# Cosine-similarity attention with hand-written engine orders: three pairs of heads normalised by head instead of both heads at once, and new orders in the last third

## The chip, the cores and the metric

The kernel runs on one core of one Trainium2 chip. The metric is the device time of one execution in microseconds (us). The engines are TensorE (PE in the profile; its weight loads are PEld), VectorE (DVE), ScalarE (ACT), GpSimd (POOL) and SyncE (SP), which issues most of the DMAs.

## The reference

```python
# Q, K, V: (batch 8, heads 12, seq 512, dim 64), f32; tau = 0.1
Q_norm = Q / (np.linalg.norm(Q, axis=-1, keepdims=True) + 1e-10)
K_norm = K / (np.linalg.norm(K, axis=-1, keepdims=True) + 1e-10)
scores = np.einsum('bhqd,bhkd->bhqk', Q_norm, K_norm) / tau
weights = np.exp(scores - np.max(scores, axis=-1, keepdims=True))
weights = weights / (np.sum(weights, axis=-1, keepdims=True) + 1e-10)
return np.einsum('bhqk,bhkd->bhqd', weights, V).astype(np.float32)
```

There are 96 heads. The scores are bounded by 1/tau, so the kernel takes no maximum; it takes the row sums from a column of ones beside V.

## The kernel before, in words

The 96 heads are worked as 48 pairs, numbered 0 to 47. Each step of the program is an operation with a key (name, pair, and further indices), the engine that runs it, and the steps that it needs. The operations are numbered in the order in which `P.add` adds them, and the table `ORDER` lists for each engine the numbers in the order in which that engine issues them. The engines run their lists strictly in order; `Program.run` turns each need into a semaphore wait. So an instruction that waits holds up everything behind it on its engine.

The steps of one pair, with the lines of the profile:

- `LD`, `LV`: loads of Q, K and V (SP, L348, L351). `VC`: cast of V, two pairs at once (POOL, L675).
- `SQ` (POOL, L374): squares of K. `SSQ` (PE, L413) sums them with identity matmuls into the free columns of a bank of `oops`, and `RED ... 1` (DVE, L426) finishes the sum. For Q the sums come from batch statistics: `RED ... 0` and `BN`, each two instructions (DVE, L393).
- `NEW g k` (DVE, L455 to L478): the inverse square roots of a group of four pairs; group 16 is pairs 36 to 39, group 17 is 40 to 43, group 18 is 44 to 47. Step 6 gives the factors of Q, step 7 those of K. `UNIT` (DVE, L488) scales the factors of Q for a pair of which one chunk is off ACT.
- `SCL s 0` (DVE, L497) and `SCL s 1` (POOL, L497): Q and K times their factors, into `qn`.
- `TR s 0`, `TR s 1` (PE, L506): four transposes each, into the bank `tps`; `EVA s` (DVE, L524) copies them to `qt`.
- `SCO s c` (PE, L642): the scores of chunk c (0 to 3) of the keys, for both heads, two matmuls; `EXP s c` (ACT, L666; L657 for the three last pieces): the exponential of 128 x 1024 elements into `et`. Two buffers of `scps` alternate, so an SCO waits for the EXP two chunks before it.
- In the pairs 25, 33, 40, 44 and 47 one chunk is off ACT. Its scores are made by `SCX s h` (PE, L582), `X s h 0` (DVE, L589) and `X s h 1` (DVE, L592, or L591 for pair 47) and then `Y s 0` to `Y s 4`, five steps on POOL (L607, L606, L612, L607, L607). In pair 47 `Y 47 h 1` (DVE, L595), `Y 47 h 2` (POOL, L596) and `Y 47 h 3` (DVE, L597) do this for each head h; both `Y 47 h 2` need both `Y 47 h 1`.
- `PV s h i` (PE, L691; L728 for pair 47): four matmuls each, the weights times V, into bank h of `oops`. The first PV of a pair in a bank waits until the NRM of the pair before has read that bank. In a pair with a chunk off ACT the last PV of each head waits for the last Y.
- `RCP s h`, `NRM s h` (DVE, L710 and L712; L739 and L741 for pair 47): the reciprocals of the row sums, and the product that divides by them, from `oops` to `ob`. `ST s` (SP, L716; L745 for pair 47) stores `ob`.

From pair 10 on, `joint(s)` makes RCP and NRM one instruction each for both heads (8 reciprocals and 512 products in each of the 128 partitions); it is false for the pairs with a chunk off ACT and for pair 47, which go by head (4 and 256). With a joint NRM both banks come free at the same moment. Every NRM waits for its RCP by a semaphore, though both run on DVE.

Of the kernel before, what the change touches and what calls it, by code (L numbers as in the profile page):

```python
# [108 lines left out]
def bass_cosine_similarity_attention_kernel(  # L109
# [138 lines left out]
    def nrm(s, h):  # L248
        return ("NRM", s, 0 if joint(s) else h) if s >= 0 else None
# [512 lines left out]
OFF = {(25, 3): (25, 25), (33, 3): (33, 33), (40, 3): (40, 40), (44, 3): (44, 44), (47, 2): (47, None)}  # L762
# [22 lines left out]
JOINT = True  # L785
RCPJ = ()
JOINT_FROM = 10
# [29 lines left out]
def joint(s):  # L817
    return JOINT and s >= JOINT_FROM and s not in {i for i, _ in OFF} and s < 47


def slack(s, most):
# [129 lines left out]
```

## Time and profile before

| | us |
|---|---|
| median of 3 runs | 187.84 |
| lowest and highest of them | 187.17 and 187.9 |
| the profiled execution | 187.44 |
| its span in the profile | 185.4 |

The profiled execution's own time is 2.0 us over its span. In the views the first column is the start in us from the span's start, the second the length; "xN" counts instructions that are merged in one row; in brackets stand the idle time in front and what ended it. In a row of the windows the stretch is followed by its length and then the busy time and the count of instructions of PE, PEld, DVE, ACT and POOL, the granted TensorE clock, the DMA share and GB/s.

### The profile page before, as it was taken

Reading aid. Unit: us, or ns where it says so; the run is one execution under the profiler, and the core shown is the slowest. Engines: PE = TensorE matmul, PEld = TensorE weight load, DVE = VectorE, ACT = ScalarE, POOL = GpSimd, SP = SyncE. Lnnn points to the kernel's source line nnn. Section 1 sums busy time; section 2 is a strip of 40 time slices with the busy share of each in tenths; the row PEclk is TensorE's granted clock in tenths of the full one; section 3 lists DMA queues with packets and bytes.
Section 4 is the critical chain, followed back from the end, with each engine's and each line's share of the span. In section 5 each row is a group of like instructions: output and inputs, shape, how many; then the busy total and the mean of one; then the engine's idle time right before and its main releaser. Section 6 shows DMA issues by size and latency. Waiting matters only on the chain.

```text
span 185.4 us, 6946 instructions
## 1 busy us (share of the span) xinstructions
PE 173.3 (93%) x2802; PEld 110.8 (60%) x2802; DVE 172.2 (93%) x613; ACT 178.2 (96%) x207; POOL 164.0 (88%) x154
## 2 busy tenths in 40 slices
PE   7689999999999999999989999999899999899882
PEld 2456666666666666666655566656566655456551
DVE  2788999999999999999999999999999999998884
ACT  4799999999999999999999999999999999999992
POOL 4699979868999988599998999999999999999950
PEclk9999999999999999999999999999999999999999
DMA  5999999999999996899999999399988422032233
GB/s 164 316 356 350 349 352 364 269 347 367 380 380 382 375 377 229 268 358 363 379 350 320 367 378 335 132 274 312 338 306 260 160 89 88 2 117 89 85 113 117
DMA packets 52448, 50.79 MB, mean 274 GB/s; under 512 B 3136, under 2 KB 52416, under 8 KB 52416
## 3 DMA queue, kind: packets, MB, share of 16 engines
q1 hardware_dynamic: 51984, 50.02, 81.4%
q8 instruction: 22, 0.36, 0.8%
q10 hardware_dynamic: 432, 0.33, 0.5%
q14 instruction: 10, 0.08, 0.1%
HBM read 37.75 MB, written 12.58 MB: 271 GB/s over the span
## 4 chain that ended last, share of the span: by engine, by line
ACT 68%; POOL 11%; DVE 8%; PE 6%; DMA 3%; issue 2%; SPq 0%; DVEq 0%; POOLq 0%
ACT et L666 67%; POOL xw L607 5%; PE oops L691 3%; DMA qk<-in_Q_dram 3%; POOL et L607 2%; DVE ob L712 2%; PE scps L642 2%; POOL qn L497 2%; POOL xw L606 1%; POOL xz L612 1%; DVE qn L497 1%; DVE qt L524 1%; DVE xz L592 1%; PE tps L506 1%; DVE xp L589 1%
## 5 line engine op out<-in xcount | busy, mean ns | idle before, releaser
L666 ACT ACTIVATE et<-scps 128x1024 bf16<-128x1024 f32 (+1 forms) x186 | 169.5, 1112 | 0.4 <-PE scps L642 0.4
L642 PE MATMUL scps<-qt 64*128 64x512 bf16 x374 | 73.5, 386 | 4.4 <-ACT et L666 2.4
L691 PE MATMUL oops<-vb,et 128*128 128x65 bf16 x1504 | 71.3, 194 | 1.0 <-POOL et L607 0.4
L691 PEld LDWEIGHTS oops<-vb,et 128*128 128x128 bf16 x1504 | 54.9, 97 | 26.5 <-issue 17.4
L497 POOL TENSOR_TENSOR qn<-qk,rk 128x512 bf16<-128x512 f32 x42 | 43.2, 1043 | 7.4 <-DVE rk L455 6.6
L374 POOL TENSOR_TENSOR sq<-qk 128x512 bf16<-128x512 f32 x34 | 34.9, 1040 | 0.7 <-DMA qk<-in_K_dram 0.7
L497 DVE TENSOR_TENSOR qn<-qk,nps 128x512 bf16<-128x512 f32 x52 | 34.6, 678 | 0.8 <-ACT nps L447 0.8
L712 DVE TENSOR_TENSOR ob<-oops,rd 128x512 f32<-128x512 f32 (+1 forms) x61 | 34.2, 563 | 0.2
L524 DVE COPY qt<-tps 128x1024 bf16<-128x1024 bf16 x47 | 32.2, 686 | 1.5 <-PE tps L506 1.1
L506 PE MATMUL tps<-ident,qn 128*128 128x128 bf16 x376 | 32.1, 220 | 0.6 <-DVE qn L497 0.5
L393 DVE BATCH_NORM_STATS2 st<-qk 128x6 f32<-128x128 f32 x136 | 31.7, 283 | 0.0
L642 PEld LDWEIGHTS scps<-qt 64*128 64x128 bf16 x374 | 18.4, 92 | 21.4 <-ACT et L666 9.1
L506 PEld LDWEIGHTS tps<-ident,qn 128*128 128x128 bf16 x376 | 21.3, 98 | 12.2 <-issue 6.1
L675 POOL TENSOR_SCALAR vb<-vf 128x1024 bf16<-128x1024 f32 (+1 forms) x29 | 26.1, 910 | 0.3
L377 POOL TENSOR_TENSOR sq<-qk 128x1024 bf16<-128x1024 f32 x10 | 18.9, 1893 | 0.3 <-DMA qk<-in_K_dram 0.3
L413 PE MATMUL oops<-sq,ident 128*128 128x64 bf16 x320 | 16.0, 193 | 0.7 <-ACT sq L366 0.4
L413 PEld LDWEIGHTS oops<-sq,ident 128*128 128x128 bf16 x320 | 11.9, 98 | 3.8 <-issue 2.0
L710 DVE RECIPROCAL rd<-oops 128x8 f32<-128x8 f32 (+1 forms) x61 | 11.4, 191 | 1.7 <-PE oops L691 0.7
L607 POOL TENSOR_TENSOR xw<-xw,xz 128x1024 f32<-128x1024 f32 x4 | 9.4, 2356 | 0.3
L607 POOL TENSOR_TENSOR et<-xw,xp 128x1024 bf16<-128x1024 f32 x4 | 8.5, 2129 | 0.2
L607 POOL TENSOR_TENSOR xw<-xz 128x1024 f32<-128x1024 f32 x4 | 7.6, 1893 | 0.5 <-DVE xz L592 0.4
L426 DVE TENSOR_REDUCE nps<-oops 128x8 f32<-128x64 f32 x36 | 7.5, 208 | 0.4 <-PE oops L413 0.4
(80 smaller groups left out, 113.0 us busy)
## 6 DMA issues: line engine op xcount, KB each, us to landing
vf<-in_V_dram SPq DMA_DIRECT2D x48, 256.0 KB, 6.5
qk<-in_Q_dram SPq DMA_DIRECT2D x47, 256.0 KB, 6.4
qk<-in_K_dram SPq DMA_DIRECT2D x47, 256.0 KB, 6.4
out_dram<-ob SPq DMA_DIRECT2D x47, 256.0 KB, 6.0
qk<-in_Q_dram SPq DMA_DIRECT2D x2, 128.0 KB, 2.6
qk<-in_K_dram ACTq DMA_DIRECT2D x2, 128.0 KB, 2.8
out_dram<-ob SPq DMA_DIRECT2D x1, 128.0 KB, 1.7
out_dram<-ob SPq DMA_DIRECT2D x1, 64.0 KB, 1.7
```

Source lines behind the costliest of these rows:

```text
L374: lambda e: e.tensor_tensor(out=sqf[:, 8 * DIM :], in0=data[:, 8 * DIM :], in1=data[:, 8 * DIM :], op=ALU.mult))
L393: last = e.bn_stats(out=st[:, g % R_X, c8 + 4 * h + t : c8 + 4 * h + t + 2, :].rearrange("p g x -> p (g x)"), in_=rows[:, t : t + 2].rearr ...
L413: last = e.matmul(out=o_ps[bank][:, at : at + 64], lhsT=ident[:, :], rhs=sq[iqs][:, 8 * w : 8 * w + 8, 8 * k : 8 * k + 8], start=(k == 0), ...
L497: lambda e, w=w, r=r: e.tensor_tensor(out=qn[iqn][:, w].rearrange("p t h d -> p h t d"), in0=qk[iq][:, w].rearrange("p h (t d) -> p h t d" ...
L506: last = e.transpose(t_ps[:, w, t, :], qn[iqn][:, w, t].rearrange("p h d -> p (h d)"), ident[:, :])
L524: lambda e, ws=ws: e.tensor_copy(out=qt[iqt][:, ws, :, :].rearrange("p w t x -> p (w t x)"), in_=t_ps[:, ws, :, :].rearrange("p w t x -> p ...
L607: mul = lambda o, x, y: lambda e: e.tensor_tensor(out=o, in0=x, in1=y, op=ALU.mult)
L642: last = e.matmul(out=sc_ps[:, 2 * b + h, :], lhsT=qt[iqt][64 * h : 64 * h + 64, 1, c, :], rhs=qt[iqt][64 * h : 64 * h + 64, 0, :, :], sta ...
L666: lambda e, c=c, b=b, hs=hs: e.activation(out=et[iet][:, c, hs[0] : hs[-1] + 1, :], in_=sc_ps[:, 2 * b + hs[0] : 2 * b + hs[-1] + 1, :], f ...
L675: return e.tensor_scalar(out=vb[:, ib // 2, :, ib % 2 : ib % 2 + n, :, 0:DIM].rearrange("p c r h d -> p (r h) c d"), in0=vf[:, iv : iv + n ...
L691: last = e.matmul(out=o_ps[h][:, 65 * t : 65 * t + 65], lhsT=et[iet][:, c, h, 128 * t : 128 * t + 128], rhs=vb[:, s % R_VB // 2, c, s % 2, ...
L712: lambda e, hs=hs, grid=grid: e.tensor_tensor(out=ob[io][:, hs], in0=grid[:, :, :, 0:DIM], in1=rd[io][:, hs, :].unsqueeze(3).to_broadcast( ...
```

## The change

The pairs 43, 45 and 46 are no longer joint: each gets two RCPs and two NRMs, one for each head, so that there are six more instructions on DVE. The numbers of the operations behind them shift, and the lists of POOL, DVE and PE are written anew from about 122 us of the profile on. The lists of ACT and SP keep their order.

```diff
 def joint(s):
-    return JOINT and s >= JOINT_FROM and s not in {i for i, _ in OFF} and s < 47
+    return JOINT and s >= JOINT_FROM and s not in {i for i, _ in OFF} and s < 43
...
     "pool": (
...
-        "1242 1352 1276 1421 1177 1518 1574 1330 1319 1291 1292 1293 1294 1295 1395 1428 1606 1639 1493 1460 1471 "
-        "1557 1727 1671 1537 1792 1613 1624 1759 1646 1581 1552 1553 1554 1555 1690 1556 1800 1734 1766 1710 1705 "
-        "1706 1707 1708 1709 1777 1811 1817 "
+        "1242 1352 1276 1421 1177 1574 1319 1330 1518 1291 1292 1293 1294 1295 1395 1606 1460 1428 1639 1471 1493 "
+        "1624 1673 1557 1537 1646 1729 1798 1581 1613 1763 1552 1553 1554 1555 1692 1556 1806 1770 1712 1736 1707 "
+        "1708 1709 1710 1711 1781 1817 1823 "
...
```

The numbers say little, so here are the parts of the lists around the steps that the prediction speaks of, written as keys.

POOL, before and after:

```text
-  SQ 40, SQ 41, VC 34, SCL 34 1, Y 33 0 .. Y 33 4, SCL 36 1, SCL 37 1, SQ 42, SQ 43, SCL 39 1, SCL 38 1,
-  VC 38, VC 40, SQ 45, SQ 44, SCL 40 1, SQ 47, SCL 42 1, VC 42, SQ 46, SCL 43 1, SCL 41 1,
-  Y 40 0 .. Y 40 3, SCL 44 1, Y 40 4, SCL 47 1, SCL 45 1, SCL 46 1, VC 44, Y 44 0 .. Y 44 4, VC 46, Y 47 0 2, Y 47 1 2
+  SQ 41, SCL 34 1, VC 34, SQ 40, Y 33 0 .. Y 33 4, SCL 36 1, SQ 42, SCL 38 1, SCL 37 1, SQ 43, VC 38,
+  SCL 39 1, VC 42, SQ 44, VC 40, SCL 40 1, SCL 43 1, SQ 45, SQ 47, SCL 41 1, SCL 42 1, SQ 46,
+  Y 40 0 .. Y 40 3, SCL 44 1, Y 40 4, SCL 47 1, SCL 46 1, VC 44, SCL 45 1, Y 44 0 .. Y 44 4, VC 46, Y 47 0 2, Y 47 1 2
```

DVE, around NEW 17 and X 40, before and after (RED 46 0 stands ahead of NEW 17 in the list after):

```text
-  EVA 38, NEW 17 4, NEW 17 3, BN 47, NEW 17 6, UNIT 40, NEW 17 7, SCL 40 0, EVA 39, RCP 36, RED 44 1, NRM 36, EVA 40,
-  SCL 41 0, X 40 0 0, RED 46 0, X 40 0 1, RCP 37, RED 45 1, NRM 37, X 40 1 0, X 40 1 1, RED 44 0, RED 47 0, RED 45 0
+  EVA 38, NEW 17 5, BN 45, NEW 17 4, NEW 17 3, BN 47, NEW 17 6, NEW 17 7, UNIT 40, EVA 39, SCL 40 0, RCP 36, RED 44 1, NRM 36, EVA 40,
+  RED 45 0, RED 44 0, X 40 0 0, RED 45 1, X 40 0 1, RCP 37, NRM 37, X 40 1 0, X 40 1 1, SCL 41 0, RED 47 0
```

DVE, the end:

```text
-  EVA 45, SCL 47 0, SCL 46 0, RCP 42, NRM 42, EVA 46, EVA 47, RCP 43, NRM 43, X 47 1 0, X 47 0 0, X 47 1 1, X 47 0 1,
-  RCP 44 1, RCP 44 0, NRM 44 1, NRM 44 0, Y 47 0 1, Y 47 1 1, RCP 45, NRM 45, Y 47 0 3, RCP 46, NRM 46, Y 47 1 3, RCP 47 0, ...
+  EVA 45, SCL 46 0, SCL 47 0, EVA 46, RCP 42, NRM 42, EVA 47, RCP 43 1, NRM 43 1, X 47 0 0, X 47 1 0, RCP 43 0, X 47 1 1, NRM 43 0, X 47 0 1, Y 47 1 1,
+  RCP 44 0, RCP 44 1, NRM 44 0, NRM 44 1, Y 47 0 1, RCP 45 0, NRM 45 0, RCP 45 1, NRM 45 1, Y 47 0 3, RCP 46 0, RCP 46 1, NRM 46 0, NRM 46 1, Y 47 1 3, RCP 47 0, ...
```

PE, around pair 40 (PV 37 1 is short for its four steps):

```text
-  SCO 38 2, PV 37 1 0, PV 37 0 0, PV 37 0 1, SCX 40 0, SCO 38 3, PV 37 1 1, PV 37 0 2, PV 37 1 2, SCO 39 0, PV 37 0 3, SSQ 45 1, PV 37 1 3, SCO 39 1, SCX 40 1,
-  SCO 39 2, PV 38 (four), SCO 39 3, PV 38 (three), SCO 40 0, SSQ 46 1, TR 41 1, PV 38 1 3, SCO 40 1, TR 41 0, SCO 40 2
+  SCO 38 2, PV 37 0 0, PV 37 1 0, PV 37 0 1, PV 37 0 2, SCX 40 0, SCO 38 3, PV 37 0 3, SSQ 45 1, SCO 39 0, PV 37 1 1, PV 37 1 2, PV 37 1 3, SCO 39 1, SCX 40 1,
+  SCO 39 2, PV 38 (four), SCO 39 3, PV 38 0 3, SSQ 46 1, PV 38 1 1 .. 1 3, SCO 40 0, TR 41 1, SCO 40 1, TR 41 0, PV 39 0 0, PV 39 0 1, SCO 40 2
```

PE, the end:

```text
-  SCO 43 1, PV 41 1 0 .. 1 2, PV 41 0 0 .. 0 2, SCO 43 2, PV 41 0 3, PV 41 1 3, SCO 43 3, TR 45, SCO 44 0, PV 42 (four), SCO 44 1, PV 42 (four), SCO 44 2, TR 46, SCO 45 0,
-  PV 43 (four), SCO 45 1, TR 47 0, TR 47 1, PV 43 (four), SCO 45 2, SCO 45 3, SCX 47 1, SCX 47 0, PV 44 1 0, SCO 46 0, PV 44 (four), SCO 46 1, PV 44 1 2, PV 44 1 3, PV 44 0 3, SCO 46 2, SCO 46 3,
-  PV 45 (both heads mixed), SCO 47 0, SCO 47 1, PV 46 (both heads mixed), SCO 47 3, PV 47
+  SCO 43 1, PV 41 0 0 .. 0 2, PV 41 1 0, SCO 43 2, PV 41 0 3, PV 41 1 1 .. 1 3, SCO 43 3, TR 45, SCO 44 0, PV 42 (three), SCO 44 1, TR 46 1, PV 42 1 2, TR 46 0, SCO 44 2, PV 42 (four), SCO 45 0,
+  TR 47 0, TR 47 1, SCO 45 1, PV 43 1 0 .. 1 3, SCO 45 2, SCX 47 0, SCX 47 1, PV 43 0 0, SCO 45 3, PV 43 0 1 .. 0 3, PV 44 1 0, SCO 46 0, PV 44 1 1, SCO 46 1, PV 44 1 2, PV 44 0 0 .. 0 2, SCO 46 2, PV 44 0 3, PV 44 1 3, SCO 46 3,
+  PV 45 0 0 .. 0 3, PV 45 1 0 .. 1 3, SCO 47 0, SCO 47 1, PV 46 0 0 .. 0 3, PV 46 1 0 .. 1 3, SCO 47 3, PV 47
```

54 rows, old and new, of the table ORDER are left out of this document.

## The prediction

> **What bounds the kernel now.** I read the page first, then the chain of waits, then each engine's timeline from 143 us on, because the changed orders begin at about 122 us. Steps are named as in the kernel's section: EXP, SCO, PV, RCP, NRM, EVA, X, Y, SCL.
>
> ```profile
> span 185.4 us, 6946 instructions
> PE 173.3 (93%) x2802; PEld 110.8 (60%) x2802; DVE 172.2 (93%) x613; ACT 178.2 (96%) x207; POOL 164.0 (88%) x154
> ACT 68%; POOL 11%; DVE 8%; PE 6%; DMA 3%; issue 2%; SPq 0%; DVEq 0%; POOLq 0%
> ```
>
> By the shares ACT (ScalarE) is the bound. The shares mix stages, so here are the windows of the last third, and ACT's timeline in pieces:
>
> ```profile
> 143.70:175.60 31.90, 30.05 (x462) 18.51 (x462) 30.20 (x82) 31.88 (x36) 31.04 (x25) 1.00 0.27 91
> 157.70 6.61 ACT L666 ACTIVATE et<-scps 128x1024 bf16<-128x1024 f32 x7
> 164.03 3.15 ACT L666 ACTIVATE et<-scps 128x1024 bf16<-128x1024 f32 x3
> 171.59 6.80 ACT L666 ACTIVATE et<-scps 128x1024 bf16<-128x1024 f32 x7
> 178.35 2.12 ACT L666 ACTIVATE et<-scps,lift_in 128x1024 bf16<-128x1024 f32 x2
> 180.66 1.42 ACT L657 ACTIVATE et<-scps,lift_in 128x512 bf16<-128x512 f32 x3 [0.19 <-PE scps L642]
> ```
>
> ACT looks full, but start to start it is not. Undisturbed, seven EXPs take 164.03 - 157.70 = 6.33, which is 0.904 each. The eight from 164.03 to 171.59 (pair 43, three of 44, one of 45) take 7.56 instead of 7.23, so 0.33 is lost. The seven to 178.35 lose 0.43 and the two to 180.66 lose 0.50. Together ACT loses 1.26 us; where the profile names a releaser, it is an SCO that TensorE (PE) issued late. So another chain paces the end, and GpSimd (POOL) and VectorE (DVE) show it:
>
> ```profile
> 145.88 1.04 POOL L497 TENSOR_TENSOR qn<-qk,rk 128x512 bf16<-128x512 f32 x1
> 150.90 2.04 POOL L497 TENSOR_TENSOR qn<-qk,rk 128x512 bf16<-128x512 f32 x2
> 153.04 1.89 POOL L607 TENSOR_TENSOR xw<-xz 128x1024 f32<-128x1024 f32 x1
> 173.49 2.13 POOL L607 TENSOR_TENSOR et<-xw,xp 128x1024 bf16<-128x1024 f32 x1
> 175.67 0.42 PE L691 MATMUL oops<-vb,et 128*128 128x65 bf16 x8 [0.37 <-POOL et L607]
> 171.87 0.69 DVE L524 COPY qt<-tps 128x1024 bf16<-128x1024 bf16 x1 [1.11 <-PE tps L506]
> 175.17 0.68 DVE L591 SCALAR_TENSOR_TENSOR yz<-tps,yp 128x512 f32<-128x512 f32 x1
> 176.00 0.30 DVE L710 RECIPROCAL rd<-oops 128x4 f32<-128x4 f32 x2
> 176.22 0.76 DVE L712 TENSOR_TENSOR ob<-oops,rd 128x256 f32<-128x256 f32 x2
> 176.89 0.69 DVE L595 SCALAR_TENSOR_TENSOR tps<-yz,yp 128x512 f32<-128x512 f32 x1
> 177.49 0.70 DVE L595 SCALAR_TENSOR_TENSOR nps<-yz,yp 128x512 f32<-128x512 f32 x1
> 178.09 0.20 DVE L710 RECIPROCAL rd<-oops 128x8 f32<-128x8 f32 x1
> 178.33 0.69 DVE L712 TENSOR_TENSOR ob<-oops,rd 128x512 f32<-128x512 f32 x1
> 179.17 1.13 PE L691 MATMUL oops<-vb,et 128*128 128x65 bf16 x32 [0.34 <-DVE ob L712]
> 180.23 0.39 PE L642 MATMUL scps<-qt 64*128 64x512 bf16 x2
> 180.58 0.69 DVE L712 TENSOR_TENSOR ob<-oops,rd 128x512 f32<-128x512 f32 x1
> 182.98 0.28 DVE L741 TENSOR_TENSOR ob<-oops,rd 128x128 f32<-128x128 f32 x1
> ```
>
> POOL is busy 31.04 of the window's 31.90 us, back to back, until Y 44 4 (173.49) ends at 175.62. PV 44 waits for it; then comes one serial chain: RCP and NRM 44, the two Y 47 steps on DVE, RCP and NRM 45, PV 46, RCP and NRM 46, PV 47, the last product at 182.98, and the last store. The changed kernel can end sooner only by a shorter chain after 175.62, or by an earlier Y 44 4; POOL's work up to there stays the same set.
>
> **The change, part by part.** *The split itself.* Three joint reciprocals and three joint products become six and six. For pair 44, which already goes by head, RCP, RCP, NRM, NRM run from 176.00 to 176.22 + 0.76 = 176.98, and the next DVE step starts 0.89 after the first. For pair 45 (joint) the two run from 178.09 to 179.02, and a step behind would start about 0.6 after 178.33, so 0.84 after the first. The price is 0.05 of engine time a pair with both heads ready. In the order RCP, NRM, RCP, NRM each NRM must wait for its own RCP; after 182.02 that took 0.22:
>
> ```profile
> 182.02 0.18 DVE L739 RECIPROCAL rd<-oops 128x4 f32<-128x4 f32 x1 [0.16 <-PE oops L728]
> 182.24 0.42 DVE L741 TENSOR_TENSOR ob<-oops,rd 128x256 f32<-128x256 f32 x1
> ```
>
> That form takes 2 x (0.22 + 0.42) = 1.28 less a few hundredths of overlap, against 0.93, so 0.05 to 0.3 a pair. The Trainium skill, Perfetto Trace Analysis, section Optimizing Scalar/DVE Operations, speaks against the split: each DVE instruction carries about 125 ns of access overhead on PSUM, so a saturated engine wants grouped operations. By that figure the six extra instructions would cost 6 x 0.125 = 0.75 us, an estimate, where the rows give 0.15 to 0.9. The rows decide what I use, and where it lies: the engine is not saturated there, since DVE idles 1.11 in front of EVA 47 (171.87) and again in the tail.
>
> *What the split buys, with the new order.* TR 47 and all of PV 42 now stand ahead of SCO 45 1 and 45 0 on PE. EXP 45 0 starts one pitch before 171.59, at 170.69, and an SCO needs 0.43 ahead of its EXP (180.23 to 180.66), so PV 42 ends by about 170.1, RCP and NRM 42 (0.93) by 171.0, and EVA 47 starts there instead of at 171.87. SCX 47 follows SCO 45 2, which goes out when EXP 45 0 ends, some 1.1 after its start, and gives DVE its input at about 172.55. DVE then has X 47 0 0, X 47 1 0, RCP 43 0, X 47 1 1, NRM 43 0, X 47 0 1 and Y 47 1 1, at 0.6 each for five (176.89 to 177.49), 0.1 for the RCP and 0.34 for the NRM: 3.45, to 176.0. That is when PV 44 delivers, so Y 47 1 1 has left the serial chain (it stood at 177.49) and NRM 44 still ends at 176.98. Then, by the same durations:
> Y 47 0 1 is issued at 176.9 and done at 177.6, so POOL's square starts 0.6 earlier. PV 45 head 0 is done at 177.6 (16 of the 32 matmuls first). RCP 45 0 starts 177.6, NRM 45 0 ends 178.25, NRM 45 1 178.8 (was 179.02). PV 46 head 0 waits only for NRM 45 0 and for SCO 47 1 in front of it on PE, which goes out when EXP 46 3 ends (171.59 + 6.80 = 178.39 now, about 0.1 earlier with SCO 46 2 in time) and takes some 0.3: it starts at 178.62 instead of 179.17, and the 32 matmuls end about 179.75. RCP 46 0 is done by then; RCP 46 1 starts 179.78, NRM 46 1 ends 180.64 (was 181.27). SCO 47 3 stands behind PV 46 on PE and moves from 180.23 to 179.7; its EXP starts two pitches after 178.35, at 180.16, instead of 180.66, and ACT ends at 180.66 + 1.42 - 0.5 = 181.58. Y 47 1 3, PV 47 and the last RCPs and NRMs follow, and the last product ends 182.6 instead of 182.98 + 0.28 = 183.26. This term is -0.6. Its bounds: -0.7 (ACT's end plus the same last steps) and -0.2, if EVA 47 stays at 171.87. Then 4.5 us of DVE steps stand in front of RCP 44, which comes 0.35 late, and -0.6 becomes about -0.2.
>
> *What the new orders cost POOL.* POOL has no slack at two places. SCL 40 1 (145.88) waits for NEW 17 7, and Y 40 0 (153.04) for X 40 1 1:
>
> ```profile
> 145.62 0.18 DVE L455 SCALAR_TENSOR_TENSOR rk<-nps,ys 128x32 f32<-128x32 f32 x1
> 152.28 0.69 DVE L592 SCALAR_TENSOR_TENSOR xz<-xp,tps 128x512 f32<-128x512 int16 x1
> 144.92 0.48 DVE L393 BATCH_NORM_STATS2 st<-qk 128x6 f32<-128x128 f32 x2
> 148.54 0.68 DVE L497 TENSOR_TENSOR qn<-qk,nps 128x512 bf16<-128x512 f32 x1
> 145.53 0.17 DVE L488 TENSOR_SCALAR nps<-nps 128x8 f32<-128x8 f32 x1
> ```
>
> NEW 17 7 ends at 145.80, and X 40 1 1 at 152.97, 0.03 after POOL's last SCL (150.90 + 2.04 = 152.94). In the new DVE order RED 46 0, a pair of statistics (0.40 start to start, from 144.92 to the next row at 145.32), is moved ahead of NEW 17 7, and UNIT 40 (0.09, from 145.53) behind it: NEW 17 7 is 0.31 later. Ahead of X 40 1 1 come RED 44 0 and RED 45 0 as well (0.80), while SCL 41 0 (148.54; 0.59 to the next row at 149.13) goes behind: 0.2 later.
>
> ```profile
> 145.32 0.18 DVE L455 SCALAR_TENSOR_TENSOR nps<-nps,ys 128x32 f32<-128x32 f32 x1
> 149.13 0.68 DVE L589 TENSOR_SCALAR xp<-tps 128x512 int16<-128x512 f32 x1
> ```
>
> The first delay, 0.3 at SCL 40 1, moves POOL so that it meets the second one at 153.24: they do not add. Everything behind on POOL keeps its set, so Y 44 4 ends 0.3 later. The other steps moved on POOL (squares, casts, SCLs) read loads and factors that are there before; SCL 45 1, one cast later, moves TR 45 1 and with it EVA 45, which has nearly 2 us left before SCO 45 0. Bounds: 0, if DVE's own waits vanish in the new order, and +0.4.
>
> *PE and ACT before the tail.* SCO 43 2, 45 2 and 46 2 lose the PVs and transposes that stood in front of them, so ACT wins back most of 0.33 + 0.43. At the other places (SCX 40 0 now waits for EVA 40, 0.4 later; SSQ 46 for a square that POOL does two steps later) ACT loses some 0.4. Both come to nothing at the end: ACT has to wait at SCO 47 0, which stands behind PV 45, which stands behind Y 44 4. SP's order and ACT's are unchanged.
>
> *Sum.* -0.6 + 0.3 = -0.3. The profiled execution took 187.44 (185.4 of span and 2.0 around it): 187.1. The three runs have their median at 187.84, 0.4 above it, and their lowest at 187.17, so against the median the same sum gives 187.5; I keep the profile's own. A measurement of this kernel tells about 0.5% (0.94 us) from no change, and -0.3 lies within.
>
> **The rivals.** *ACT is the bound.* Then every late EXP that goes is won: -1.26, to 186.2. For it speak 96%; against it, that ACT's losses in the last two pieces end on NRM 45 and Y 44 4. The Trainium skill, Perfetto Trace Analysis, section Identifying the Most-Contended Engine, says the engine of highest occupancy is to be followed and its gaps closed; that would be this rival. Chance 0.12.
>
> *POOL starves at Y 40 0.* The new PE order puts SCX 40 0 in front of SCO 38 3 and SSQ 45 1 in front of SCO 39 0, and the new DVE order keeps RCP 37 and NRM 37 in front of X 40 1:
>
> ```profile
> 147.93 0.69 DVE L524 COPY qt<-tps 128x1024 bf16<-128x1024 bf16 x1
> 148.68 0.39 PE L582 MATMUL tps<-qt 64*128 64x512 bf16 x1
> 150.71 0.20 DVE L710 RECIPROCAL rd<-oops 128x8 f32<-128x8 f32 x1
> ```
>
> EVA 40 (147.93) ends 148.6 and goes to 149.0, past the old start of SCX 40 0 (148.68). My walk has PV 37 done at 150.7 and DVE at RCP 37 at 150.9. If PE loses 0.2 more there, PV 37 misses its place before the next SCO, and PE's slots come once in an EXP: 0.90. X 40 1 1, Y 40 0 and Y 44 4 come 0.9 later: 187.44 - 0.3 + 0.9 = 188.0. Pair 44 repeats the pattern, with RCP 40 and NRM 40 between the X 44 steps, so a PE that is a slot behind is likely to miss there too; a second slot at Y 44 0 gives 188.9. For it: DVE and PE wait on each other three times within 3 us. Against it: 0.2 of margin, and POOL's waits from 120 us on show one alone, in the tail:
>
> ```profile
> POOL yz L596 <- DVE nps L595: 1.5, 1, 1.5
> ```
>
> Chance 0.28: 0.08 for one slot, 0.20 for two.
>
> *The forecast* has 0.60.
>
> **How the numbers follow.** 187.1 is the likeliest. One slot (188.0) is still within 0.5% of 187.44, so no difference gets 0.60 + 0.08 = 0.68, faster 0.12, slower 0.20. The range runs from 186.4 (187.1 with the tail at -0.7, POOL at 0, and a few tenths of the first rival) to 188.9; it leaves out most of the first rival and what exceeds two slots. The likeliest case alone: 186.7 (-0.7) to 187.6 (-0.2 and +0.4).
>
> **What would show it.** Right: NEW 17 7 ends near 146.1 and SCL 40 1 starts near 146.2; Y 44 4 ends at 175.9; Y 47 1 1 is done before RCP 44; PV 46 starts 0.3 earlier than 179.17 (0.55 less 0.27), and the last product ends near 182.9. Wrong: idle time on POOL between 146 and 176 beyond 0.3; RCP 44 behind a late Y 47 1 1; or Y 44 4 on time and an end that is lower by over 0.9, which would make ACT the bound.

## The result, and the profile after

| | before | after |
|---|---|---|
| median, us | 187.33 | 187.83 |
| lowest to highest, us (22 runs each) | 187.10 to 190.03 | 187.52 to 189.45 |
| profiled execution, us | 187.44 | 188.12 |
| its span, us | 185.4 | 186.2 |

The ratio after to before is 1.0032, with a 95% interval of 1.0019 to 1.0044. So the changed kernel is slower by 0.32%, 0.6 us, where 0.3 us less was forecast. The difference is within the 0.5% that the prediction counts as no difference, and 187.83 lies inside its range, but the sign is the other one.

The page of the changed kernel, its span, engines and the shares of the chain that ended last:

```profile
span 186.2 us, 6951 instructions
PE 174.2 (94%) x2802; PEld 110.9 (60%) x2802; DVE 173.6 (93%) x619; ACT 177.9 (96%) x207; POOL 164.1 (88%) x154
ACT 84%; PE 6%; DMA 3%; POOL 3%; DVE 1%; issue 1%; SPq 1%; DVEq 0%; POOLq 0%
```

DVE has its six more instructions and 1.4 us more busy time (172.2 before). That is more than the 0.15 to 0.9 us at which the prediction priced the three splits, so some other DVE instruction has probably become longer. The chain's share on ACT, 84% for 68%, tells little: chains of nearly one length lie beside each other, and the view follows the one that ended last.

Before the times can be compared, one offset has to be taken out. POOL's timeline just ahead of the first changed order, first of the kernel before, then of the changed one:

```profile
117.78 3.04 POOL L497 TENSOR_TENSOR qn<-qk,rk 128x512 bf16<-128x512 f32 x3
```

```profile
118.00 3.04 POOL L497 TENSOR_TENSOR qn<-qk,rk 128x512 bf16<-128x512 f32 x3
```

The profiled execution of the changed kernel is 0.22 us late before anything in it differs. All that follows is therefore measured from a fixed point inside the kernel: the end of Y 44 4 on POOL, from which the prediction's serial chain starts. POOL's timeline at the tail of the changed kernel:

```profile
173.72 2.13 POOL L607 TENSOR_TENSOR et<-xw,xp 128x1024 bf16<-128x1024 f32 x1
175.93 1.06 POOL L675 TENSOR_SCALAR vb<-vf 128x1024 bf16<-128x1024 f32 x1
179.10 2.04 POOL L596 TENSOR_TENSOR yz<-yz 128x512 f32<-128x512 f32 x2 [2.10 <-DVE rd L710]
```

Y 44 4 starts at 173.72, 55.72 after the row at 118.00; before, it starts at 173.49, 55.71 after the row at 117.78. POOL has lost nothing. It ends at 175.85, and from here to the end of the last product the kernel before took 183.26 - 175.62 = 7.64 us. The changed one takes 184.09 - 175.85 = 8.24. The difference is +0.60, which is the whole measured loss. DVE's timeline shows where it arises:

```profile
174.63 0.41 DVE L712 TENSOR_TENSOR ob<-oops,rd 128x256 f32<-128x256 f32 x1
174.96 0.68 DVE L591 SCALAR_TENSOR_TENSOR yz<-tps,yp 128x512 f32<-128x512 f32 x1
175.95 1.58 DVE L595 SCALAR_TENSOR_TENSOR nps<-yz,yp 128x512 f32<-128x512 f32 x1 [0.31 <-POOL et L607]
177.45 0.24 DVE L710 RECIPROCAL rd<-oops 128x4 f32<-128x4 f32 x2
177.65 0.76 DVE L712 TENSOR_TENSOR ob<-oops,rd 128x256 f32<-128x256 f32 x2
178.33 0.69 DVE L595 SCALAR_TENSOR_TENSOR tps<-yz,yp 128x512 f32<-128x512 f32 x1
180.17 0.69 DVE L597 SCALAR_TENSOR_TENSOR et<-yz,tps 128x512 bf16<-128x512 f32 x1
183.81 0.28 DVE L741 TENSOR_TENSOR ob<-oops,rd 128x128 f32<-128x128 f32 x1
```

The third row is Y 47 1 1. It was in front of RCP 44 as intended, but it waited 0.31 us for POOL's Y 44 4, and then took 1.58 us instead of 0.70. It ended at 177.53, 0.54 after VC 46 on POOL (175.93 + 1.06 = 176.99). RCP 44 followed at 177.45, 1.60 after Y 44 4's end; before, it stood 0.38 behind it. The chain of waits of the changed kernel in order of time has the same place in two rows, and puts the extra time down to nothing that it can name:

```profile
175.95 0.53 DVE nps L595
176.48 0.97 issue
177.45 0.24 DVE rd L710 x2
...
178.13 1.15 PE oops L691 x32
179.28 0.34 PE scps L642 x2
179.62 0.02 issue
179.65 2.12 ACT et L666 x2
181.76 1.31 ACT et L657 x3
```

PE and ACT pass the delay on (their timelines): PV 45 waits for NRM 44, and SCO 47 0, behind PV 45, leaves ACT idle for 1.28 us.

```profile
178.13 1.15 PE L691 MATMUL oops<-vb,et 128*128 128x65 bf16 x32 [1.16 <-DVE ob L712]
179.65 2.12 ACT L666 ACTIVATE et<-scps,lift_in 128x1024 bf16<-128x1024 f32 x2 [1.28 <-PE scps L642]
```

So RCP 44 comes 1.60 - 0.38 = 1.22 us later, and from there to the end it takes 184.09 - 177.45 = 6.64 us instead of 183.26 - 176.00 = 7.26. The end of the chain has another course than the forecast's sum: it goes from PV 45 over SCO 47 0 and ACT's last five EXPs, and not over PV 46 and NRM 46. The new tail is 0.62 shorter, and 1.22 - 0.62 = 0.60.

### The profile page after: what moved, and what is told of

Same layout as the page of the kernel before. It is cut to its first block, busy times and chain, and to the rows that moved or that the text cites. A ratio compares the mean times of both kernels' runs of the same rounds, so it can differ in the third digit from the quotient of the medians.

```text
span 186.2 us, 6951 instructions
## 1 busy us (share of the span) xinstructions
PE 174.2 (94%) x2802; PEld 110.9 (60%) x2802; DVE 173.6 (93%) x619; ACT 177.9 (96%) x207; POOL 164.1 (88%) x154
## 4 chain that ended last, share of the span: by engine, by line
ACT 84%; PE 6%; DMA 3%; POOL 3%; DVE 1%; issue 1%; SPq 1%; DVEq 0%; POOLq 0%
ACT et L666 83%; DMA qk<-in_K_dram 3%; PE oops L691 3%; PE scps L642 2%; POOL xw L607 1%; POOL et L607 1%; PE tps L506 1%; ACT et L657 1%; SPq L345 0%; PE tps L582 0%; POOL sq L368 0%; DVE nps L595 0%; ACT ys L444 0%; SPq L348 0%; PE oops L413 0%
## 5 line engine op out<-in xcount | busy, mean ns | idle before, releaser
L712 DVE TENSOR_TENSOR ob<-oops,rd 128x256 f32<-128x256 f32 (+1 forms) x64 | 34.7, 544 | 0.3
L710 DVE RECIPROCAL rd<-oops 128x4 f32<-128x4 f32 (+1 forms) x64 | 11.8, 188 | 1.6 <-PE oops L691 0.6
```

The source lines that it names most:

```text
L712: lambda e, hs=hs, grid=grid: e.tensor_tensor(out=ob[io][:, hs], in0=grid[:, :, :, 0:DIM], in1=rd[io][:, hs, :].unsqueeze(3).to_broadcast( ...
```

## The experiments

**The theory:** Y 47 1 1 takes both of its tensor inputs from SBUF (`yz`, `yp`), and such a DVE instruction stands still while a POOL instruction that reads SBUF runs. Put directly behind Y 44 4, it meets VC 46, the cast of V. **The rivals:** the late RCP 44 is only a matter of order (anything put in front of it costs its length); the split itself costs the time; the new orders ahead of the tail cost it. All changes are made in the changed kernel (after) or in the kernel before, as named; ratios are to the kernel before, run on the same chip in the same series.

| kernel | median, us | ratio, 95% interval | RCP 44 behind Y 44 4's end | last product's end behind it | against 7.64 |
|---|---|---|---|---|---|
| before | 187.33 | | 0.38 | 7.64 | |
| after | 187.83 | 1.0032, 1.0019 to 1.0044 | 1.60 | 8.24 | +0.60 |
| e1_y_back | 187.33 | 0.9991, 0.9977 to 1.0005 | 0.49 | 7.29 | -0.35 |
| e2_y_psum | 186.98 | 0.9971, 0.9956 to 0.9985 | 0.71 | 7.36 | -0.28 |
| e3_y_front | 188.98 | 1.0074, 1.0049 to 1.0098 | 1.60 | 8.74 | +1.10 |
| e4_split_only | 187.10 | 0.9974, 0.9952 to 0.9996 | 0.39 | 7.21 | -0.43 |
| e5_middle_only | 187.24 | 0.9998, 0.9988 to 1.0007 | 0.39 | 7.65 | +0.01 |
| e6_cast_waits | 187.06 | 0.9988, 0.9977 to 0.9999 | 0.71 | 7.37 | -0.27 |
| e7_tail | 187.23 | 0.9982, 0.9969 to 0.9995 | 0.47 | 7.41 | -0.23 |
| e8_no_need | 189.09 | 1.0086, 1.0063 to 1.0109 | 2.63 | 9.84 | +2.20 |
| e9_split_heads | 187.54 | 1.0008, 0.9995 to 1.0021 | 0.39 | 7.96 | +0.32 |
| e10_split_45 | 187.22 | 0.9993, 0.9979 to 1.0008 | 0.39 | 7.37 | -0.27 |
| e11_split_43_46 | 187.10 | 0.9968, 0.9940 to 0.9996 | 0.38 | 7.48 | -0.16 |

The last three columns come from one profiled execution each; the before and after rows stand as examples of how they are worked out. An interval times 187.4 holds the last column in every row but e8's (+1.2 to +2.0 by the runs).

**e1: Y 47 1 1 back behind Y 47 0 1** (in after, DVE's list):

```diff
-  Y 47 1 1, RCP 44 0, RCP 44 1, NRM 44 0, NRM 44 1, Y 47 0 1,
+  RCP 44 0, RCP 44 1, NRM 44 0, NRM 44 1, Y 47 0 1, Y 47 1 1,
```

> The changed kernel with one DVE step moved: Y 47 1 1 goes back behind Y 47 0 1, where POOL's cast VC 46 is over. Theory 1 (DVE's Y 47 1 1, which reads two tensors of SBUF, stands still while POOL's VC 46 runs): Y 47 1 1 takes 0.7 us instead of 1.58, RCP 44 starts about 0.1 after PV 44 ends instead of 1.0 after, and the kernel gains some 0.8 us on the changed one, to 0.2 to 0.3 us below the kernel before. Theory 2 (the six added instructions and their waits are the loss): still 0.4 to 0.6 us slower than the kernel before.

DVE's timeline of it: RCP 44, and both Y 47 h 1 behind it at 0.69 us.

```profile
176.16 0.31 DVE L710 RECIPROCAL rd<-oops 128x4 f32<-128x4 f32 x2 [0.69 <-PE oops L691]
177.05 0.69 DVE L595 SCALAR_TENSOR_TENSOR tps<-yz,yp 128x512 f32<-128x512 f32 x1
177.65 0.69 DVE L595 SCALAR_TENSOR_TENSOR nps<-yz,yp 128x512 f32<-128x512 f32 x1
```

This one move takes back the loss: 0.9991 against 1.0032. The split and every other new order are still in, so they don't cost the time. It doesn't yet tell the length of the moved step from the standstill.

**e2: the same place, one input from PSUM.** In after, `Y 47 h 1` reads its first input from its own PSUM bank instead of `yz`, so one chunk of pair 47 is computed from other data; order, needs and size stay.

```diff
-e.scalar_tensor_tensor(out=b_ps, in0=yz[:, h, :], scalar=-a2,
+e.scalar_tensor_tensor(out=b_ps, in0=b_ps, scalar=-a2,
```

> The changed kernel in its own order, but both Y 47 h 1 read the PSUM bank in place of the SBUF tile yz as their first input, so that only one input lies in SBUF; this changes what is computed for one chunk of pair 47. Theory 1 (two SBUF inputs against a running POOL instruction): Y 47 1 1 takes 0.7 us beside VC 46, RCP 44 starts near 0.65 after Y 44 4 ends instead of 1.6 after, and the kernel is 0.7 to 0.9 us faster than the changed one, 0.1 to 0.3 below the kernel before. Theory 2 (Y 47 1 1 waits for something else, or the added instructions cost): its record keeps 1.58 us and the kernel stays 0.4 to 0.6 us above the kernel before.

Its DVE timeline, then its POOL timeline:

```profile
175.74 0.70 DVE L595 SCALAR_TENSOR_TENSOR nps<-nps,yp 128x512 f32<-128x512 f32 x1 [0.31 <-POOL et L607]
```

```profile
175.72 1.06 POOL L675 TENSOR_SCALAR vb<-vf 128x1024 bf16<-128x1024 f32 x1
```

The two still start together, and the step takes 0.70 us instead of 1.58. The need of Y 44 4 still holds it back (0.31), and RCP 44 still comes 0.71 behind Y 44 4. The kernel is faster than before, by 0.29%. So the second SBUF input is what lengthens the step; a matter of order alone would have left the 1.58 us.

**e6: the cast is made to wait.** In after, VC 46 gets one more need, so that POOL is idle while Y 47 1 1 runs:

```diff
-  [("LV", s + i) for i in range(n)] + [key("PV", ...
+  [("LV", s + i) for i in range(n)] + ([("Y", 47, 1, 1)] if s == 46 else []) + [key("PV", ...
```

> The changed kernel with one need added: POOL's VC 46 waits for Y 47 1 1, so that the two cannot run at once; no order changes. Theory 1 (port): Y 47 1 1 takes 0.7 us, VC 46 starts near 0.7 after Y 44 4 instead of 0.1, RCP 44 comes 0.9 us sooner than in the changed kernel; Y 47 0 1 may still meet the end of VC 46 and take up to 1.0 us. The kernel is 0.6 to 0.9 us faster than the changed one, 0 to 0.3 below the kernel before. Without the port as cause it is equal to the changed kernel or slower by up to 0.7 (VC 46 later).

Its DVE timeline, then its POOL timeline:

```profile
175.67 0.70 DVE L595 SCALAR_TENSOR_TENSOR nps<-yz,yp 128x512 f32<-128x512 f32 x1 [0.32 <-POOL et L607]
177.17 1.00 DVE L595 SCALAR_TENSOR_TENSOR tps<-yz,yp 128x512 f32<-128x512 f32 x1
```

```profile
176.56 1.07 POOL L675 TENSOR_SCALAR vb<-vf 128x1024 bf16<-128x1024 f32 x1 [0.99 <-DVE rd L710]
```

With its two SBUF inputs untouched, Y 47 1 1 takes 0.70 us when POOL is idle. The moved cast now meets Y 47 0 1 instead: that one ends at 178.17, 0.54 after the cast's end (177.63), as Y 47 1 1 did in the changed kernel.

**e3: the move alone, in the kernel before.** The old orders, and Y 47 1 1 put in front of RCP 44:

```diff
-  RCP 44 1, RCP 44 0, NRM 44 1, NRM 44 0, Y 47 0 1, Y 47 1 1, RCP 45, NRM 45,
+  Y 47 1 1, RCP 44 1, RCP 44 0, NRM 44 1, NRM 44 0, Y 47 0 1, RCP 45, NRM 45,
```

> The kernel before with one DVE step moved: Y 47 1 1 in front of RCP 44 1, as in the changed kernel; no split and no other order. Theory 1: Y 47 1 1 starts within 0.1 us of VC 46 and takes about 1.5 us; RCP 44 comes 1.0 to 1.3 us later than before and the end 0.5 to 0.9 us later (0.6 comes back because the step has left the chain behind). Theory 2: Y 47 1 1 takes 0.7 us, and the kernel is within 0.2 us of the kernel before.

Its DVE timeline:

```profile
175.88 1.57 DVE L595 SCALAR_TENSOR_TENSOR nps<-yz,yp 128x512 f32<-128x512 f32 x1
177.37 0.24 DVE L710 RECIPROCAL rd<-oops 128x4 f32<-128x4 f32 x2
```

The move alone makes the step 1.57 us long and RCP 44 1.22 later. The end comes 1.10 later in the profile and 1.4 us by the runs (0.9 to 1.8), more than I expected: the old tail behind RCP 44 takes 7.14 us here where the changed kernel's takes 6.64. The 1.4 holds something else as well: in three of the six runs the mean granted clock of TensorE was 0.991 instead of 1.000, and they took 189.23 to 189.28 where the others took 188.47 to 188.74.

**e8: the step earlier still.** In after, Y 47 1 1 goes directly behind X 47 1 1, and its need of Y 44 4 is dropped:

```diff
-  X 47 1 1, NRM 43 0, X 47 0 1, Y 47 1 1, RCP 44 0,
+  X 47 1 1, Y 47 1 1, NRM 43 0, X 47 0 1, RCP 44 0,
-  [("X", s, h, 1)] + [("Y", i, 4) for i in held[-1:]]
+  [("X", s, h, 1)] + [("Y", i, 4) for i in held[-1:] if not h]
```

> The changed kernel with Y 47 1 1 moved up behind X 47 1 1 and without its need of Y 44 4, so that it meets POOL's Y 44 4, a product of two tensors, in the middle. Theory 1 (a DVE step with two SBUF inputs stands still until the running POOL instruction is over): Y 47 1 1 starts about 0.9 us after Y 44 4 and ends about 0.5 after Y 44 4's end (1.7 us), or, if VC 46 gets its turn first, 0.5 after VC 46's end (2.8 us); the kernel is 0.2 to 1.5 us slower than the kernel before. If only the cast VC 46 disturbed it: Y 47 1 1 takes 0.7 us and the kernel is 0.2 to 0.5 us faster than the kernel before.

Its DVE timeline, then its POOL timeline:

```profile
174.37 1.67 DVE L595 SCALAR_TENSOR_TENSOR nps<-yz,yp 128x512 f32<-128x512 f32 x1
```

```profile
173.35 2.13 POOL L607 TENSOR_TENSOR et<-xw,xp 128x1024 bf16<-128x1024 f32 x1
175.57 1.39 POOL L675 TENSOR_SCALAR vb<-vf 128x1024 bf16<-128x1024 f32 x1
```

The partner is now Y 44 4: the step ends at 176.04, 0.56 after Y 44 4's end (175.48). And now POOL stands still in its turn: VC 46, which starts while the step is still at work, takes 1.39 us instead of 1.06. NRM 43, behind the step on DVE, comes late, PV 44 with it, and the loss is the largest of all.

Not all of the +2.20 is due to the two lengthened steps directly. PE is idle for 1.42 us in front of PV 44's last matmuls, and from 176.5 to 180 us the windows give it a granted clock of 0.50 to 0.54 of full speed, with 1.00 on both sides. PE's timeline shows PV 45 in this stretch, at 1.61 us instead of the 1.15 in the changed kernel:

```profile
178.89 1.61 PE L691 MATMUL oops<-vb,et 128*128 128x65 bf16 x32
```

Of the four runs, the two at a mean clock of 0.989 and 0.991 took 189.43 (the profiled one) and 189.50, the two at 0.999 took 188.32 and 188.75.

**e4: the split alone.** The kernel before with its orders, and only the three joint pairs split:

```diff
-  RCP 43, NRM 43 ... RCP 45, NRM 45 ... RCP 46, NRM 46
+  RCP 43 0, RCP 43 1, NRM 43 0, NRM 43 1 ... (and so 45 and 46)
```

> The kernel before with the split alone: pairs 43, 45 and 46 by head, RCP, RCP, NRM, NRM in the place of the joint two; all other orders as before. Theory 1: the split costs 0.05 us a pair on DVE and the heads' banks come free at nearly the same time, so 0 to 0.2 us slower than the kernel before. Theory 2 (the added instructions are the loss): 0.5 us slower.

Its DVE timeline (NRM 45, and the last product), then PE's (PV 46):

```profile
178.22 0.76 DVE L712 TENSOR_TENSOR ob<-oops,rd 128x256 f32<-128x256 f32 x2
182.46 0.28 DVE L741 TENSOR_TENSOR ob<-oops,rd 128x128 f32<-128x128 f32 x1
```

```profile
178.79 1.14 PE L691 MATMUL oops<-vb,et 128*128 128x65 bf16 x32
```

I had the sign wrong: the split is worth 0.26% (0.04 to 0.48) by itself. RCP and NRM 45 together run 178.01 to 178.98, 0.97 instead of 0.93, so the price was right; but the first bank comes free with the first NRM, and PV 46 starts 3.26 behind Y 44 4's end (175.53) instead of 3.55. What it follows then is SCO 47 1, the step in front of it on PE. By 0.9974/1.0032 this kernel is 0.6% ahead of the changed one.

**e10 and e11: which pair's split.** The kernel before with pair 45 alone split, and with 43 and 46 (in the list of DVE the RCPs and NRMs stand as in e4):

```diff
-  s not in {i for i, _ in OFF} and s < 47
+  s not in {i for i, _ in OFF} and s < 47 and s != 45             # e10
+  s not in {i for i, _ in OFF} and s < 47 and s not in (43, 46)   # e11
```

> The kernel before, with only pair 45 split (RCP, RCP, NRM, NRM). The split of all three pairs in the old orders gave 0.9974. If it gives by the bank that comes free earlier (PV 46 head 0 waits for NRM 45 head 0 alone: 178.79 there, 179.17 before), nearly all of it is pair 45's: ratio about 0.998, PV 46 near 178.8, last product ending 0.3 to 0.5 earlier than before. If the gain came from another pair or from earlier stages, ratio 1.000 and PV 46 near 179.2.

> The kernel before, with pairs 43 and 46 split and 45 joint. By the theory that the gain is pair 45's: ratio 1.000 (0.999 to 1.001), PV 46 near 179.17 as before; the split of 46 lets the first PV 47 of one bank start some 0.3 earlier, but the last product needs both banks and Y 47 1 3, which stands behind both NRM 46 and comes 0.05 later. By the rival (46 frees PV 47): ratio 0.998, the PV 47 group's wait for NRM 46 (0.48 before) gone.

PE's timeline of e10 (PV 46), then of e11 (PV 46, and PV 47 in the banks of `oops`):

```profile
179.55 1.14 PE L691 MATMUL oops<-vb,et 128*128 128x65 bf16 x32
```

```profile
179.54 1.13 PE L691 MATMUL oops<-vb,et 128*128 128x65 bf16 x32 [0.33 <-DVE ob L712]
181.28 0.93 PE L728 MATMUL oops<-vb,et 128*128 128x65 bf16 x20
```

In e10 Y 44 4 ends at 176.29, so PV 46 is 3.26 behind it, as in e4. In e11 it keeps its wait for NRM 45, but the wait of PV 47 for NRM 46 (0.48 before) is gone. The profiles give -0.27 and -0.16 us, together e4's -0.43, so by them both kernels gain by a bank that comes free earlier. Pair 43 isn't tested apart from 46, but RCP 44 stands 0.38 behind Y 44 4's end as before, so its split doesn't show in the tail. That pair 45 has nearly all of the gain, as I expected, isn't borne out, and the runs can't rank the two, as their intervals overlap.

**e5: the new orders ahead of the tail, alone.** No split; DVE's list new up to EVA 47, PE's up to SCO 45 1, POOL's whole; then the old ones.

```diff
-  joint up to 46, old lists
+  joint up to 46, new lists for POOL, for DVE to EVA 47, for PE to SCO 45 1
```

> The new orders up to EVA 47 on DVE, SCO 45 1 on PE and to the end on POOL; from there the order of the kernel before, with joint RCPs and NRMs. It holds everything that the prediction charged to POOL (+0.3) and what ACT wins in the middle. Theory 1 (the loss is the port alone, POOL's chain to Y 44 4 unchanged): Y 44 4 ends within 0.1 us of where it ends in the kernel before, counted from a common row, and the time is within 0.2 us of the kernel before. The prediction's POOL term: 0.3 us slower. The rival that ACT is the bound: 0.3 to 0.7 us faster.

Its ACT timeline, to be held against the pieces that the prediction shows:

```profile
171.73 6.90 ACT L666 ACTIVATE et<-scps 128x1024 bf16<-128x1024 f32 x7
178.62 2.12 ACT L666 ACTIVATE et<-scps,lift_in 128x1024 bf16<-128x1024 f32 x2
```

The ratio is 0.9998 (0.9988 to 1.0007). Y 44 4 ends at 175.85 here, 0.23 later than before. With that taken out, the seven EXPs start 0.09 earlier (171.73 against 171.59), and the two of pair 47 0.04 later (178.62 against 178.35): what little ACT has won by the new orders up to here, it has lost again by EXP 47 0. POOL's term of 0.3 isn't there either: Y 44 4 starts 55.69 after the row that begins at 118.03 in e5, where it was 55.71 before.

**e7 and e9: the tail by head on PE.** e7 is e1 with the reciprocals of 45 ahead of its products, with RCP, NRM, RCP, NRM for 46, and with SCO 47 0 and SCO 47 3 between the heads of PV 45 and PV 46. e9 is e4 with the same on PE (head 1 of 45 first):

```diff
-  PV 45 (both heads mixed), SCO 47 0, SCO 47 1, PV 46 (both heads mixed), SCO 47 3
+  PV 45 1 (four), SCO 47 0, PV 45 0 (four), SCO 47 1, PV 46 0 (four), SCO 47 3, PV 46 1 (four)   # e9
```

> The changed kernel with a new tail: on DVE Y 47 1 1 behind Y 47 0 1, RCP 45 0, RCP 45 1, NRM 45 0, NRM 45 1 for pair 45 and RCP, NRM, RCP, NRM for pair 46; on PE SCO 47 0 stands between the heads of PV 45 and SCO 47 3 between the heads of PV 46. If the port is avoided, the bound of the tail is ACT's last EXPs, and they start about 0.3 to 0.5 us sooner than with Y 47 1 1 moved back alone: 0.4 to 0.7 us faster than the kernel before. If the chain over NRM 46 and PV 47 is the bound instead: equal to the kernel with Y 47 1 1 moved back alone, 0.1 to 0.2 below the kernel before.

> The split in the old orders, and PE's list at the end by head: four PVs of one head of 45, SCO 47 0, the other four, SCO 47 1, four PVs of 46 head 0, SCO 47 3, the other four. If the end is set by ACT's last pieces, SCO 47 0 out 0.5 earlier takes EXP 47 0 with it and the ratio falls to 0.995; if by the chain over NRM 45, PV 46, NRM 46, Y 47 1 3 and PV 47, the scores in front of the second heads push that chain back by 0.2 to 0.4 and the ratio is 0.998 to 1.001. I expect the second, by what the tail by head gave before (EXP 47 3 0.4 earlier, the end unchanged).

DVE's timeline of e9 (RCP 45, and the second RCP 46), then the last three EXPs on ACT's timeline, first of e9, then of e4:

```profile
178.22 0.25 DVE L710 RECIPROCAL rd<-oops 128x4 f32<-128x4 f32 x2 [0.36 <-PE oops L691]
180.61 0.18 DVE L710 RECIPROCAL rd<-oops 128x4 f32<-128x4 f32 x1 [0.72 <-PE oops L691]
```

```profile
180.02 1.42 ACT L657 ACTIVATE et<-scps,lift_in 128x512 bf16<-128x512 f32 x3
```

```profile
180.30 1.42 ACT L657 ACTIVATE et<-scps,lift_in 128x512 bf16<-128x512 f32 x3
```

ACT's last pieces start 4.73 behind Y 44 4's end (175.29) in e9. That is 0.31 earlier than before (5.04), and yet the last product comes 0.32 later. But most of the 0.31 is the split's: in e4, from which e9 differs on PE alone, they start at 4.77 (180.30 - 175.53). The order on PE brings ACT 0.04 and costs 0.75 at the end (7.96 for 7.21): the scores in front of the second heads delay RCP 45 and RCP 46, and with them PV 46 and PV 47. The clearer case is e7. There the pieces start at 180.12, 4.43 behind Y 44 4's end where e1's start 4.86 behind it, and the end is no better than e1's within the intervals (0.9982 and 0.9991). From the start of these EXPs to the end of the last product it is 2.44 us in e4 and in the changed kernel, 2.98 in e7 and 3.23 in e9: in these two the end no longer waits for ACT, but for the chain over RCP 46 and Y 47 1 3. The two chains lie within a few tenths of each other, and shortening one at the other's cost brought nothing.

## Why the prediction was wrong, and where it was right

**What bounds the kernel** was right in its place and incomplete in its course. The stretch from Y 44 4's end on carries the measured difference of each kernel but e8, whose profiled run had the low clock. But its last part is two chains of nearly one length, over NRM 46 and over ACT's last five EXPs; the prediction's sum followed the first and took the second for a bound, and the changed kernel ends on the second.

**The walk to the tail** was right to 0.1 us, with the offset of 0.23 at Y 44 4 taken out: EVA 47 starts at 171.23 - 0.23 = 171.00 (171.0 was forecast), X 47 0 0 at 172.48 (172.55). Without its wait Y 47 1 1 would have started 0.60 after X 47 0 1, at 175.56, and been done at 176.02 on that clock, where 176.0 was said, if nothing had run beside it; but Y 44 4 runs until 175.85 there, and e8 shows what meeting it costs.

**The step that failed** is the sentence that Y 47 1 1 "has left the serial chain", as one of five steps at 0.6 each. Two things were missed there. Its need of Y 44 4 stands in the code (`("Y", i, 4) for i in held[-1:]`), so it could not start before 175.85; even without the standstill RCP 44 then stands 0.71 instead of 0.38 behind Y 44 4 (e2, e6), +0.33. Of this 0.22 is the need's; in e1, with the step at its old place, RCP 44 is at 0.49 already, since in the new order of PE SCO 46 2 stands in front of the last PV 44. And its price was read off rows in which POOL was not at work on anything beside it: at 176.89 in the kernel before, the first of these steps starts 0.13 after VC 46 ends. POOL's timeline of the kernel before shows that both of these steps (176.89 to 178.19) lie between its instructions:

```profile
175.70 1.06 POOL L675 TENSOR_SCALAR vb<-vf 128x1024 bf16<-128x1024 f32 x1
178.27 2.04 POOL L596 TENSOR_TENSOR yz<-yz 128x512 f32<-128x512 f32 x2 [1.51 <-DVE nps L595]
```

Beside VC 46 the step took 1.58 instead of 0.70, and RCP 44 came at 1.60 instead of 0.71, +0.89. Together that is the 1.22 by which RCP 44 is late. Had the price of the step been right, the sum would have been -0.6 + 0.33 = -0.27, which is what the profiles of e2 and e6 show at -0.28 and -0.27.

**The tail's own term** came out at its size: from RCP 44 to the end -0.62 was measured for the -0.6 forecast. That is partly luck, as the end has another course, and the moved step has little share in it. With the step back at its old place this stretch takes 7.29 - 0.49 = 6.80 us in e1, and with the split alone 7.21 - 0.39 = 6.82 in e4, against 7.26 before and 6.64 in the changed kernel. So the move is worth some 0.16 of the 0.62, no more than the 0.22 that its need costs even without the standstill.

The rows of the kernel before could not show the standstill, since neither step meets it there. The Trainium skill, SBUF — State Buffer, section Who interferes with whom, says that a DVE instruction with two SBUF inputs contends with a GpSimd instruction that reads SBUF, and that the pair of ports that they share is an exclusive lock: whichever is issued first has it for the whole instruction, and the other is fully blocked. The traces agree: 1.58 against 0.70 us, ending 0.54 to 0.56 after POOL's instruction in four kernels, and 1.39 against 1.06 us the other way round in e8. The prediction did name the sign ("RCP 44 behind a late Y 47 1 1"), without giving it a mechanism or a chance.

**POOL's term of +0.3** was 0: the lower of its bounds held, "0, if DVE's own waits vanish in the new order". NEW 17 7, in DVE's timeline of the changed kernel:

```profile
145.36 0.49 DVE L393 BATCH_NORM_STATS2 st<-qk 128x6 f32<-128x128 f32 x2
145.76 0.19 DVE L455 SCALAR_TENSOR_TENSOR nps<-nps,ys 128x32 f32<-128x32 f32 x1
145.85 0.19 DVE L455 SCALAR_TENSOR_TENSOR rk<-nps,ys 128x32 f32<-128x32 f32 x1
```

It ends at 146.04, and 145.81 with the offset of 0.23 out, where it ended at 145.80 before. In the new order statistics and EVA 38 stand between small steps that need each other. Before, two such steps back to back started 0.21 apart (NEW 17 6 and UNIT 40, 145.32 to 145.53); in the new order NEW 17 6 and NEW 17 7, which don't need each other, start 0.09 apart (145.76 to 145.85). That this makes up all of the 0.3 isn't shown. The forecasts of 146.1 for NEW 17 7 and of 175.9 for the end of Y 44 4 fit the raw times (146.04 and 175.85) by the offset alone, which is luck.

**The split** was priced rightly as engine time (0.04 us for pair 45), and the 0.75 us that the prediction estimated from the figure of the Trainium skill, Perfetto Trace Analysis, section Optimizing Scalar/DVE Operations, did not show: DVE is busy 172.4 us in e4 and 172.2 before. Its benefit by the bank that comes free earlier was in the walk, but counted with the new order; e4 shows that it needs no new order.

**The rivals.** That every late EXP would be won is refuted by e7, where ACT's last pieces come 0.43 us earlier than in e1 and the end does not follow. Nor did the 1.26 come true, as ACT's timeline of e1 shows, which has all the new orders but for one step:

```profile
171.55 6.65 ACT L666 ACTIVATE et<-scps 128x1024 bf16<-128x1024 f32 x7
178.37 2.12 ACT L666 ACTIVATE et<-scps,lift_in 128x1024 bf16<-128x1024 f32 x2 [0.17 <-PE scps L642]
```

The seven EXPs take 6.65 instead of 6.80, and EXP 47 0 then waits for SCO 47 0 and starts 2.70 behind Y 44 4's end (175.67), against 2.73 before. The prediction had this right where it let ACT's gains come to nothing at SCO 47 0. POOL starving at Y 40 0 did not happen (POOL's start of Y 44 4 keeps its distance to 0.01 us). The case that came, a slower kernel by a lengthened DVE step, was none of the rivals.

## What to carry to other kernels

An instruction's duration is a property of its place as well as of its shape: before an instruction that reads two tensors from SBUF on DVE is moved, look at what POOL runs at the new time, and price it at POOL's remaining length plus most of its own (0.54 to 0.56 of 0.70 us here). Read the needs of a moved step in the code as well, for a need that cost nothing at the old place is in no view of the profile; here it costs 0.22 us, as much as the move saves or more (some 0.16). And compare two profiles from a fixed event inside the kernel, not from the span's start: here the start was off by 0.22 us, a third of the effect.

## What the runs showed of the hardware

The standstill is not shown as a wait: the blocked DVE instruction is shown as busy for 1.58 us, and the chain of waits books 0.97 us of it as issue. It goes by inputs, not by the engine pair as such. In the changed kernel Y 47 0 3, with one input in SBUF and one in PSUM, ran at 180.17 beside the second square of POOL (179.10 to 181.14) and took 0.69 us; X 47 0 1 ran at 174.96 beside Y 44 4 and took 0.68. It works in both directions, on DVE (1.57 to 1.67 us for 0.70, and 1.00 where only the end of VC 46 is met) and on POOL (1.39 for 1.06). Whether VC 46 ahead of the Y 44 steps would free the place altogether wasn't tried.
